# A two-layer MoE trunk: expert weights loaded as 8 KB runs per partition, features folded by four

## The chip, the cores and the metric

The kernel runs on one core of a Trainium2 chip. The metric is the device time of one execution in microseconds (us); the kernel before takes 935.08 us, the median of three runs between 932.46 and 935.89 us.

## The reference, cut to what matters

256 tokens of width 1024 (float32) pass two layers. Each has a token mixer (stick-breaking attention in layer 0, retention in layer 1) and then a mixture of experts (MoE) with 16 experts; every one of the four sublayers is modulated by a conditioning vector and closed by a layer norm:

```python
shift, scale, gate = adaln_params(c, ada_w[i, 1], ada_b[i, 1])      # silu(c) @ w + b, split in 3
h = x * (1.0 + scale) + shift
logits = h @ router_w + router_b                                    # 16 experts in 4 groups of 4
...                                                                 # best group, its top 2, softmax
for e in range(16):
    hidden = silu(h @ w_gate[e]) * (h @ w_up[e])                    # 1024 -> 512
    out = out + combine[:, e:e+1] * (hidden @ w_down[e])            # 512 -> 1024
x = layer_norm(ALPHA * x + (1.0 + gate) * out, ln_g[i, 1], ln_b[i, 1])
```

The weights of all 16 experts are read in each layer: 16 x 3 matrices of 2 MB, 96 MB a layer.

## The kernel before, in words

**Stages.** The program runs stick-breaking attention, MoE of layer 0 (180 to 447 us of the trace), retention and MoE of layer 1 (660 to 918 us). Tokens lie on the 128 partitions in two blocks b. `res` holds the residual.

**An MoE.** Each expert takes up to 64 tokens; the experts are worked in eight pairs p, and both experts of a pair (u = 0, 1) stand in the two column halves of TensorE (`py[64*u:64*u+64]`), so that two matmuls run side by side. For a pair, `gather` picks its tokens out of `xn` with one-hot matmuls (L859), giving their features on the partitions (`xg`, eight tiles of 128 features, modulated by L424 and L425); `up` (matmuls L902) makes the gate and then the up product; L926 and L930 make silu(gate) x up in `mosg`; `turn` (L937) transposes it to `hidT`, four tiles of 128 hidden features; the down product (L957) is made in two halves j of 512 output columns, each in its own `py`; L962 weighs it by the router's weight and the adaLN gate into `moy`, L354 and L355 split that into two float32r parts `moyh` and `moyl`, and `scatter` (L974) puts them back to the token rows by one-hot matmuls, which `accumulate` (L462) adds to `res`. Scatters are held in a list: that of j = 0 is popped at the end of its own pair, that of j = 1 after the next pair's gate product. After pair 1 both are made at once, and `spill` asks with an If (L789, L790) if any expert has more than 64 tokens; only then it loops over the experts.

**Loads.** SyncE's queue (SP) issues nearly all DMAs in the order of the program. `load` (L155 to L161) brings 1 MB into a ring slot as [128 partitions][4][512]: row 128k + p of a 512 x 512 piece goes to partition p, so a partition gets four runs of 2 KB from four places. A pair takes 12 such loads: four each for gate, up and down. The last pair loads its last halves in smaller pieces (`mixed`). A slot is loaded again as soon as its last matmul is done.

**Around it.** `vectors` (L188 to L201) loads the small vectors at the program's start, between the second and the third load of `ada_w`. `ada_part` (L246 to L272) makes the adaLN vectors: L254 multiplies by `ada_w`, L266 turns the row into columns. `logits` transposes `res` (L310) for the router product (L318). `norm` (L486) makes `xn` on ScalarE (ACT), `applied` (L502, L503) scales it into `res`, `gate_row` (L329) and `row_ps` (L212) spread a column vector over all rows.

Of the kernel before, what the change touches and what calls it, by code (L numbers as in the profile page):

```python
# [36 lines left out]
# low part of a phase, tag: (buffers, floats per partition), in the order in which they lie in SBUF  # L37
# [3 lines left out]
# tag: its buffers as (slot of 2048 floats, offset); without an offset the buffer is the whole slot  # L41
# [47 lines left out]
def tile_trunk(ctx, tc, x, c, positions, ada_w, ada_b, ln_g, ln_b, sb_w_in, sb_w_out, ret_w_in, ret_gn_g,  # L89
# [13 lines left out]
    def ps(shape=(P, 512), tag="ps"):  # L103
# [4 lines left out]
            "dy": "t2", "rank": "pc", "ang": "t2", "crow": "sb", "spu": "t2"}  # L108
# [46 lines left out]
    def load(src):  # L155
        tag = state["ring"][state["at"] % len(state["ring"])]
        state["at"] += 1
        t = wp.tile([P, 4, 512], F32, tag="w", name=nm("w")) if tag == "w" else slot(tag, [P, 4, 512])
        if src is not None:
            SY.dma_start(t, src.rearrange("(k p) f -> p k f", p=P))  # L160
        return t  # L161

# [23 lines left out]
    col = keep([P, 176], "col")  # L186

    def vectors():  # L188
# [9 lines left out]
        SY.dma_start(wr, router_w.rearrange("(k p) e -> p k e", p=P))  # L198
# [4 lines left out]
    def gcol(i):  # L203
        return col[:, 96 + 8 * i:104 + 8 * i]

    def bcol(i):
        return col[:, 128 + 8 * i:136 + 8 * i]
# [33 lines left out]
    sums = {}  # L241

    def ada_part(i, j, on_pe):
# [19 lines left out]
        def rest():  # L263
            tp = ps([P, 4, 2], "po" if state["name"] == "RETEN" else "ps")
            for q in range(4):
                T.matmul(tp[:, q, :], e[:, q * P:(q + 1) * P], part if on_pe else ones[:, 0:2], start=(q == 0), stop=(q == 3))  # L266
            V.tensor_tensor(sums[i][:, 4 * j:4 * j + 4], tp[:, :, 0],
                            col[:, 24 * i + 4 * j:24 * i + 4 * j + 4], op=OP.add)
            if j >= 2:
                V.tensor_scalar(sums[i][:, 4 * j:4 * j + 4], sums[i][:, 4 * j:4 * j + 4], 1.0, None, op0=OP.add)  # L270
        return rest

    def ada_mod(i):
# [4 lines left out]
        V.tensor_tensor(mod[:, 8:16], gcol(i - 1), m2[:, 8:16], op=OP.mult)  # L278
        V.tensor_tensor(mod[:, 0:8], bcol(i - 1), m2[:, 8:16], op=OP.mult)
# [17 lines left out]
    def logits(st, ws, side):  # L297
# [5 lines left out]
        with urgent():  # L303
            for b in range(NB):
                for j in range(2):
                    hT = big([P, 4, P], "hT")
                    with tc.issue_after(state["end"]):
                        for q in range(4):
                            k = 4 * j + q
                            T.transpose(zs[b][j][:, q], res[:, b, k * P:(k + 1) * P], ident)  # L310
# [15 lines left out]
    def gate_row(i, tag="ps"):  # L326
        gate = tmp([P, D], "gate", 1)
        for j in range(2):
            A.activation(gate[:, j * 512:(j + 1) * 512], row_ps(sums[i][:, 16 + 4 * j:20 + 4 * j], tag),  # L329
                         AF.Copy)  # L330
# [147 lines left out]
    def norm(i, xn, mom, n=1, ahead=1):  # L478
        parts = [slice(q * D // n, (q + 1) * D // n) for q in range(n)]
        for b, (m, r) in enumerate(mom):  # L480
# [3 lines left out]
            for q in parts:  # L484
                if b < ahead:
                    last = A.activation(xn[b][:, q], res[:, b, q], AF.Identity, scale=r, bias=off)  # L486
                else:
                    last = V.tensor_scalar(xn[b][:, q], res[:, b, q], m, r, op0=OP.subtract, op1=OP.mult)
# [5 lines left out]
    def affine(i, xn, j, g, o):  # L494
        return applied(xn, j, side_row(gcol(i), j, g), side_row(bcol(i), j, o))

    def applied(xn, j, g, o):
        js = slice(j * 512, (j + 1) * 512)

        def apply():  # L500
            for b in range(NB):
                V.scalar_tensor_tensor(res[:, b, js], xn[b][:, js], ALPHA, g, op0=OP.mult, op1=OP.mult)  # L502
# [285 lines left out]
    def spill(l, xn, sc, sh, over, flag, gate):  # L788
        fv = nc.values_load(flag[0:1, 0:1], skip_runtime_bounds_check_because="only compared with zero")  # L789
        with tc.If(fv > 0):  # L790
            hT = big([P, NK, P], "sphT")
            for b in range(NB):
# [6 lines left out]
                with tc.For_i(0, NE, 1) as e:  # L799
                    def dyn(w, r0, c0):  # L800
                        t = big([P, 1, 512], "dy")
                        G.dma_start(t, w[l, bass.ds(e, 1), r0:r0 + P, c0:c0 + 512].rearrange(
                            "e (k p) f -> p (e k) f", p=P))
                        return t

                    def up(w):
                        o = ps()
                        for k in range(NK):
                            t = dyn(w, P * k, 0)
# [27 lines left out]
    def moe(l, i, xn, sc, sh, L, st, after, spare):  # L837
        with tc.issue_after(state["end"]):
            scaled = [affine(i - 1, xn, 1, ps(), ps())]
# [4 lines left out]
        with tc.issue_after(counted):  # L844
            scaled.append(applied(xn, 0, g, side_row(bcol(i - 1), 0, ps(tag="row"))))
# [36 lines left out]
        def both(w, p, rows, js, mixed):  # L882
            w = w[l, 2 * p:2 * p + 2, rows, js]
            if not mixed:
                return [[t[:, f, :] for f in range(4)] for t in (load(w[u]) for u in range(2))]
            ts = [[], []]
            for g in ([[0, 1]], [[2], [3]]):
                t = load(None)
                for n, f in enumerate(g):
                    d = t[:, 2 * n:2 * n + 2 * len(f), :].rearrange("p (u f) c -> p u f c", u=2)  # L890
                    for u in range(2):
                        SY.dma_start(d[:, u], w[u, f[0] * P:f[-1] * P + P, :].rearrange("(f p) c -> p f c", p=P))
                        ts[u].extend(d[:, u, i, :] for i in range(len(f)))
            return ts

        def up(w, p, xg, kt, o=None, mixed=False):
            o = o or ps()
            ts = both(w, p, slice(512 * kt, 512 * kt + 512), slice(0, 512), mixed)
# [19 lines left out]
        for p in range(NE // 2):  # L918
# [7 lines left out]
            A.activation(sgt, pg, AF.Silu)  # L926
# [3 lines left out]
            V.tensor_tensor(sgt, sgt, pu, op=OP.mult)  # L930
# [15 lines left out]
            for j in range(2):  # L946
                js = slice(j * 512, (j + 1) * 512)
                with urgent() if last and j else nullcontext():
                    py = ps()
                    ts = both(moe_w_down, p, slice(0, 512), js, last and j)  # L950
                    for f in range(4):
# [135 lines left out]
```

## Time and profile before

| | us |
|---|---|
| median of three runs | 935.08 (932.46 to 935.89) |
| the profiled execution: span | 928.9 |
| around the span, in the median run | 6.2 |
| TensorE (PE) busy | 884.7 (95% of the span) |
| VectorE (DVE) / ScalarE (ACT) busy | 503.8 / 264.0 |
| DMA | 305.81 MB, mean 329 GB/s |

The span is the time from the first to the last instruction of the profiled execution. The profile gives no device time for that execution itself; the 6.2 us are the difference of the median and the span. A float32 matmul on 512 columns appears as two rows of the trace, a float32r one as one.

### The profile page before, as it was taken

What the parts mean: (1) busy time and instruction counts of PE and PEld (TensorE: products, weight loads), DVE (VectorE), ACT (ScalarE), POOL (GpSimd) and SP (SyncE); (2) the same over time, 40 slices, a digit from 0 to 9 for tenths busy, and PEclk for the clock granted to TensorE, in tenths of its full rate; (3) what the DMA queues carried; (4) which work ended last, traced back from release to release, by engine and by line L of the source; (5) the groups of instructions that cost most, each with busy time, mean ns of one, the idle gap of its engine ahead of it and who ended that gap; (6) DMA issues with size and microseconds to landing.
All of it is one profiled execution on the core that took longest, in us unless ns stands there. A gap on an engine that the chain in (4) does not pass through costs nothing. (4 is left out here: it accounts for less than half of the span.)

```text
span 928.9 us, 11845 instructions
## 1 busy us (share of the span) xinstructions
PE 884.7 (95%) x4687; PEld 552.5 (59%) x4687; DVE 503.8 (54%) x958; ACT 264.0 (28%) x393; POOL 22.1 (2%) x46
## 2 busy tenths in 40 slices
PE   5899999999989999999899999999999899999994
PEld 2598887674434444344778888888944444344431
DVE  1488899635233335333797899748634422343226
ACT  1446646132111111011445434446211111111110
POOL 1000000000000000000000110030000000000000
PEclk9999999999999999999999999999899999999997
DMA  8999998899999999999469878859669999999951
GB/s 305 388 386 386 326 326 305 289 384 378 379 386 386 387 386 387 386 387 386 159 214 346 296 249 309 320 206 350 242 222 373 387 385 386 386 386 386 386 188 46
DMA packets 155378, 305.81 MB, mean 329 GB/s; under 512 B 6521, under 2 KB 6961, under 8 KB 155313
## 3 DMA queue, kind: packets, MB, share of 16 engines
q1 hardware_dynamic: 155312, 304.96, 90.3%
q8 instruction: 39, 0.64, 0.3%
q14 instruction: 27, 0.21, 0.1%
HBM read 303.89 MB, written 1.05 MB: 328 GB/s over the span
## 5 line engine op out<-in xcount | busy, mean ns | idle before, releaser
L902 PE MATMUL ps<-s,xg 128*64 128x512 f32 x544 | 154.4, 603 | 2.5 <-DVEq L790 1.4
L902 PE MATMUL ps<-w,xg 128*64 128x512 f32 x480 | 138.5, 596 | 1.4 <-DVEq L790 1.4
L355 DVE TENSOR_TENSOR wp<-w,wp 128x1024 fp32r<-128x1024 f32 x68 | 82.9, 1221 | 24.1 <-ACT wp L354 24.1
L354 ACT ACTIVATE wp<-w 128x1024 fp32r<-128x1024 f32 x68 | 71.4, 1056 | 81.7 <-PE ps L376 78.2
L902 PEld LDWEIGHTS ps<-s,xg 128*64 128x64 f32 x544 | 45.4, 138 | 73.3 <-issue 68.2
L902 PEld LDWEIGHTS ps<-w,xg 128*64 128x64 f32 x480 | 42.3, 137 | 67.4 <-issue 64.5
L425 ACT ACTIVATE xg<-ps,mod 128x128 f32<-128x128 f32 x64 | 29.3, 457 | 173.7 <-PE ps L859 147.1
L957 PE MATMUL ps<-s,hidT 128*64 128x512 f32 x272 | 75.6, 596 | 2.4 <-ACT xg L425 0.8
L462 DVE TENSOR_TENSOR res<-res,ps 128x512 f32<-128x512 f32 x64 | 41.3, 684 | 67.0 <-PE ps L974 66.7
L259 DVE SCALAR_TENSOR_TENSOR s<-w,cact,s 128x512 f32<-128x512 f32 x104 | 77.1, 747 | 0.8
L930 DVE TENSOR_TENSOR mosg<-mosg,ps 128x512 f32<-128x512 f32 x16 | 11.0, 688 | 114.7 <-PE ps L902 114.7
L859 PEld LDWEIGHTS ps<-oneh,xn 128*128 128x128 f32 x512 | 59.8, 192 | 16.2 <-issue 14.6
L957 PE MATMUL ps<-w,hidT 128*64 128x512 f32 x240 | 67.7, 595 | 1.7 <-DVE hidT L940 1.1
L859 PE MATMUL ps<-oneh,xn 128*128 128x128 f32 x512 | 65.0, 279 | 0.0
L375 PE MATMUL ps<-wp,hh 128*128 128x512 f32 (+1 forms) x144 | 56.6, 394 | 0.0
L376 PE MATMUL ps<-wp,hl 128*128 128x512 f32 x144 | 55.2, 388 | 0.0
L374 PE MATMUL ps<-wp,hh 128*128 128x512 f32 (+1 forms) x144 | 53.4, 397 | 0.7 <-ACT wp L354 0.7
L424 DVE TENSOR_SCALAR xg<-ps,mod 128x128 f32<-128x128 f32 x64 | 26.2, 409 | 50.4 <-ACT xg L425 50.3
L354 ACT ACTIVATE moyh<-moy 128x512 fp32r<-128x512 f32 x32 | 20.1, 630 | 106.8 <-DVE moy L962 106.8
L962 DVE SCALAR_TENSOR_TENSOR moy<-ps,cs,gate 128x512 f32<-128x512 f32 x32 | 24.0, 751 | 48.1 <-PE ps L957 48.1
L957 PEld LDWEIGHTS ps<-s,hidT 128*64 128x64 f32 x272 | 24.0, 137 | 38.3 <-issue 35.6
L926 ACT ACTIVATE mosg<-ps 128x512 f32<-128x512 f32 x16 | 9.6, 597 | 118.3 <-PE ps L902 118.3
(324 smaller groups left out, 1459.6 us busy)
## 6 DMA issues: line engine op xcount, KB each, us to landing
w<-in_ada_w SPq DMA_DIRECT2D x46, 1024.0 KB, 7.4
s<-in_moe_w_gate SPq DMA_DIRECT2D x34, 1024.0 KB, 14.1
s<-in_moe_w_up SPq DMA_DIRECT2D x32, 1024.0 KB, 14.0
w<-in_moe_w_gate SPq DMA_DIRECT2D x30, 1024.0 KB, 14.1
w<-in_moe_w_down SPq DMA_DIRECT2D x30, 1024.0 KB, 13.2
s<-in_moe_w_down SPq DMA_DIRECT2D x30, 1024.0 KB, 13.2
w<-in_moe_w_up SPq DMA_DIRECT2D x28, 1024.0 KB, 13.2
w<-in_ret_w_in SPq DMA_DIRECT2D x24, 1024.0 KB, 7.2
```

Of the source, the lines that this page charges most:

```text
L259: V.scalar_tensor_tensor(e, wt[:, kk, :], cact[:, k:k + 1], e, op0=OP.mult, op1=OP.add)
L354: A.activation(hi, src, AF.Copy)
L355: return V.tensor_tensor(lo, src, hi, op=OP.subtract).ins
L374: T.matmul(dst, lh, rh, start=start, stop=False)
L375: T.matmul(dst, lh, rl, start=False, stop=False)
L376: state["mm"] = T.matmul(dst, ll, rh, start=False, stop=stop).ins
L424: return V.tensor_scalar(dst, src, sc[:, k:k + 1], sh[:, k:k + 1], op0=OP.mult, op1=OP.add).ins
L425: return A.activation(dst, src, AF.Identity, scale=sc[:, k:k + 1], bias=sh[:, k:k + 1]).ins
L462: V.tensor_tensor(res[:, b, js], res[:, b, js], add, op=OP.add)
L859: T.matmul(gp[:, kk, :], xn[b][:, k * P:(k + 1) * P], oneh[:, b].rearrange("p e s -> p (e s)"), start=(kk == 0 and b == 0), stop=(kk == 3 ...
L902: state["mm"] = T.matmul(o[64 * u:64 * u + 64, :], xg[:, k, u * CAP:(u + 1) * CAP], ts[u][kk], start=(k == 0), stop=(k == NK - 1)).ins
L957: state["mm"] = T.matmul(py[64 * u:64 * u + 64, :], hidT[:, f, u * CAP:(u + 1) * CAP], ts[u][f], start=(f == 0), stop=(f == 3)).ins
```

## The change

The gate and up weights of a pair (all but the last pair's up) are loaded with four consecutive matrix rows on one partition: feature 4p + f of a group of 512 lies on partition p, as one run of 8 KB. The contraction of a matmul then runs over every fourth feature, and everything else that meets these features is folded by four in the same way: the columns of scale, shift and norm in the MoE's adaLN vectors (`fcol`, loaded by three more small DMAs and turned by four more transposes), the router's rows, the transposes of `res` (which read every fourth float), `xn`, and the `mosg` that the down product takes. The non-last down products are loaded by whole rows, two rows on a partition as [128][2][1024], and both column halves j are worked in turn from each piece. Both scatters of a pair are held until the whole gate product of the next pair is done. The diff, cut to its core:

```diff
-    def load(src):
+    def load(src, rows="(k p) f -> p k f", shape=(P, 4, 512)):
...
+        if src is not None and rows is None:
+            SY.dma_start(t.rearrange("p f c -> p (f c)"), src)
+        elif src is not None:
+            SY.dma_start(t, src.rearrange(rows, p=P))
...
+    def folded(a, n=4):
+        return a.rearrange("p (f q) -> p q f", q=n)
...
+        wide = big([P, 512], "wide")[0:40, :]
+        for r0, a in ((0, ada_b), (24, ln_g), (32, ln_b)):
+            n = 24 if r0 == 0 else 8
+            SY.dma_start(wide[r0:r0 + n, :], a.rearrange("l s (t f) -> (l s t) f", f=512))
+        cf = ps([P, 4, 40])
+        for q in range(4):
+            T.transpose(cf[:, q, :], folded(wide)[:, q, :], ident[0:40, 0:40])
+        V.tensor_copy(fcol.rearrange("p r q -> p q r"), cf)
...
-                T.matmul(tp[:, q, :], e[:, q * P:(q + 1) * P], part if on_pe else ones[:, 0:2], start=(q == 0), stop=(q == 3))
+                T.matmul(tp[:, q, :], folded(e)[:, q, :] if i % 2 else e[:, q * P:(q + 1) * P],
+                         part if on_pe else ones[:, 0:2], start=(q == 0), stop=(q == 3))
...
-                            T.transpose(zs[b][j][:, q], res[:, b, k * P:(k + 1) * P], ident)
+                            T.transpose(zs[b][j][:, q], folded(res[:, b, 512 * j:512 * j + 512])[:, q, :], ident)
...
+                    last = A.activation(to(xn[b][:, q]), of(res[:, b, q]), AF.Identity, scale=r, bias=off)
...
+                    V.scalar_tensor_tensor(folded(res[:, b, js]), xn[b][:, js].rearrange("p (q f) -> p q f", q=4), ALPHA,
+                                           folded(g), op0=OP.mult, op1=OP.mult)
...
+        def whole(w, p, kt):
+            return [[t[:, f, :] for f in range(4)] for t in
+                    (load(w[l, 2 * p + u, 512 * kt:512 * kt + 512, :].rearrange("(p f) c -> p (f c)", p=P), None)
+                     for u in range(2))]
...
+            sgf = sgt.rearrange("p (q f) -> p f q", q=4)
+            A.activation(sgf, pg.rearrange("p (f q) -> p f q", q=4), AF.Silu)
...
+            if not last:
+                pys = [ps() for _ in cols]
+                for h in range(2):
+                    ts = [load(moe_w_down[l, 2 * p + u].rearrange("(p f) c -> p (f c)", p=P)[:, 2048 * h:2048 * h + 2048],
+                               None, (P, 2, 1024)) for u in range(2)]
+                    for py, js in zip(pys, cols):
+                        for i in range(2):
+                            f = 2 * h + i
+                            for u in range(2):
+                                state["mm"] = T.matmul(py[64 * u:64 * u + 64, :], hidT[:, f, u * CAP:(u + 1) * CAP],
+                                                       ts[u][:, i, js], start=(f == 0), stop=(f == 3)).ins
+                for j in range(2):
+                    weighed(pys[j], cols[j], j)
...
+            for j in range(2 if last else 0):
```

In the changed kernel `load` stands at L155 to L165, the gate and up matmuls at L945, the down matmuls at L1020 and the scatter at L1004. Not in the diff's core: `norm` makes two pieces of 512 for each block instead of one of 1024, the silu and its product are written with a stride of 128 elements, and `spill`'s loop loads folded rows too.

TensorE's order at the change from one pair to the next (pair 2 to pair 3 of the first MoE). L957 is the down product, L902 the next pair's gate, L974 the scatter; `moyh` and `moyl` are the two parts of a half's weighed product. Before:

```order
L957 MATMUL ps_2393<-s_2396,hidT_2338 64x512
L974 MATMUL ps_2412<-moyh_2389,pt_2336 128x512
L974 MATMUL ps_2413<-moyh_2389,pt_2336 128x512
L902 MATMUL ps_2420<-s_2421,xg_2341 64x512
...
L902 MATMUL ps_2420<-s_2423,xg_2341 64x512
L974 MATMUL ps_2412<-moyl_2390,pt_2336 128x512
L974 MATMUL ps_2413<-moyl_2390,pt_2336 128x512
L902 MATMUL ps_2420<-s_2433,xg_2341 64x512
...
L974 MATMUL ps_2445<-moyh_2408,pt_2336 128x512
L974 MATMUL ps_2446<-moyh_2408,pt_2336 128x512
L974 MATMUL ps_2445<-moyl_2409,pt_2336 128x512
L974 MATMUL ps_2446<-moyl_2409,pt_2336 128x512
L902 MATMUL ps_2455<-w_2456,xg_2341 64x512
```

The same place in the changed kernel, where L1020, L945 and L1004 are the down product, the gate and the scatter:

```order
L1020 MATMUL ps_2387<-s_2402,hidT_2350 64x512
L945 MATMUL ps_2424<-s_2425,xg_2353 64x512
...
L945 MATMUL ps_2424<-s_2439,xg_2353 64x512
L1004 MATMUL ps_2449<-moyh_2414,pt_2348 128x512
L1004 MATMUL ps_2450<-moyh_2414,pt_2348 128x512
L1004 MATMUL ps_2449<-moyl_2415,pt_2348 128x512
L1004 MATMUL ps_2450<-moyl_2415,pt_2348 128x512
L1004 MATMUL ps_2457<-moyh_2420,pt_2348 128x512
L1004 MATMUL ps_2458<-moyh_2420,pt_2348 128x512
L1004 MATMUL ps_2457<-moyl_2421,pt_2348 128x512
L1004 MATMUL ps_2458<-moyl_2421,pt_2348 128x512
L945 MATMUL ps_2467<-w_2468,xg_2353 64x512
```

The eight scatter matmuls, which stood in three groups of 2, 2 and 4 around the two halves of the gate product, stand in one group behind it. This holds at the five changes from pair 0 to 1 and 2 to 6; at 6 to 7 the first two groups are joined, and from pair 1 to 2 (the If) nothing moves.

The down product of pair 1, the one before the If, whose two tiles (the first name of a row) are the two column halves. Before:

```order
L957 MATMUL ps_1957<-s_1958,hidT_1921 64x512
...
L957 MATMUL ps_1957<-w_1960,hidT_1921 64x512
L957 MATMUL ps_1976<-s_1977,hidT_1921 64x512
...
L957 MATMUL ps_1976<-s_1979,hidT_1921 64x512
L974 MATMUL ps_1995<-moyh_1972,pt_1919 128x512
```

The same in the changed kernel:

```order
L1020 MATMUL ps_1969<-s_1971,hidT_1933 64x512
...
L1020 MATMUL ps_1970<-w_1973,hidT_1933 64x512
L1020 MATMUL ps_1969<-s_1983,hidT_1933 64x512
...
L1020 MATMUL ps_1969<-s_1985,hidT_1933 64x512
L1020 MATMUL ps_1970<-s_1983,hidT_1933 64x512
...
L1020 MATMUL ps_1970<-s_1985,hidT_1933 64x512
L1004 MATMUL ps_2007<-moyh_1997,pt_1931 128x512
```

The first half was done after 8 of these 16 matmuls and is now done after 12.

The issues on SP's queue at the program's start; before:

```order
L160 DMA w_106<-in_ada_w 128x4x512
L189 DMA s_80<-in_ln_g 32x128
L190 DMA s_80<-in_ln_b 32x128
L191 DMA s_80<-in_ret_gn_g 16x128
L196 DMA con<-in_const 128x436
L197 DMA posi<-in_positions 128x2x1
L198 DMA wr<-in_router_w 128x8x16
L199 DMA rb<-in_router_b 128x16
L160 DMA w_134<-in_ada_w 128x4x512
```

And in the changed kernel:

```order
L162 DMA w_107<-in_ada_w 128x4x512
L197 DMA s_80<-in_ln_g 32x128
L198 DMA s_80<-in_ln_b 32x128
L199 DMA s_80<-in_ret_gn_g 16x128
L207 DMA s_121<-in_ada_b 24x512
L207 DMA s_121<-in_ln_g 8x512
L207 DMA s_121<-in_ln_b 8x512
L212 DMA con<-in_const 128x436
L213 DMA posi<-in_positions 128x2x1
L214 DMA wr<-in_router_w 128x2x64
L215 DMA rb<-in_router_b 128x16
L162 DMA w_145<-in_ada_w 128x4x512
```

Three more DMAs (L207) stand between the second and the third load of `ada_w`. Beyond that SP's order is the same as before.

## Rows read from the trace of the kernel before

**Rows 1.** The page's busy times, and two of the rows of its 40 equal slices (23.2 us each): the DMA engines' share in tenths and the GB/s.

```profile
PE 884.7 (95%) x4687; PEld 552.5 (59%) x4687; DVE 503.8 (54%) x958; ACT 264.0 (28%) x393; POOL 22.1 (2%) x46
...
DMA  8999998899999999999469878859669999999951
GB/s 305 388 386 386 326 326 305 289 384 378 379 386 386 387 386 387 386 387 386 159 214 346 296 249 309 320 206 350 242 222 373 387 385 386 386 386 386 386 188 46
```

**Rows 2.** TensorE's waits over the whole program: what waited for what, us in total, times, longest. The list has 19 rows.

```profile
PE ps L254 <- DMA w<-in_ada_w: 6.4, 5, 4.0
PE ps L266 <- ACT s L261: 5.0, 7, 0.8
PE ps L177 <- DMA s<-in_c: 3.2, 1, 3.2
PE ps L902 <- DVEq L790: 2.8, 2, 1.4
```

**Rows 3.** The page's two groups of gate and up matmuls, and the larger of the two groups of down matmuls: busy us, mean ns of one, and idle time of TensorE just before them with what ended most of it.

```profile
L902 PE MATMUL ps<-s,xg 128*64 128x512 f32 x544 | 154.4, 603 | 2.5 <-DVEq L790 1.4
L902 PE MATMUL ps<-w,xg 128*64 128x512 f32 x480 | 138.5, 596 | 1.4 <-DVEq L790 1.4
...
L957 PE MATMUL ps<-s,hidT 128*64 128x512 f32 x272 | 75.6, 596 | 2.4 <-ACT xg L425 0.8
```

**Rows 4.** The end of the first MoE: the timeline of SP (start, length, how many) with the issue of its last loads; the DMA issues between 396 and 414 us (median us from issue to landing); and the timeline of TensorE with the last eight down matmuls.

```profile
408.92 4.05 SPq L892 DMA_DIRECT2D s<-in_moe_w_down  x5
...
s<-in_moe_w_down SPq DMA_DIRECT2D x4, 256.0 KB, 10.7
...
436.46 1.94 PE L957 MATMUL ps<-s,hidT 128*64 128x512 f32 x8
```

**Rows 5.** The chain of waits through the change from one pair to the next in the second MoE (start us, us, what, how many rows), and from an earlier stretch of the same chain 32 float32 rows in one run.

```profile
778.15 7.02 PE ps L902 x32
...
789.73 7.09 PE ps L957 x32
796.81 0.66 PE ps L974 x2
797.48 3.58 PE ps L902 x16
801.06 0.66 PE ps L974 x2
801.72 3.58 PE ps L902 x16
805.31 1.14 PE ps L974 x4
```

**Rows 6.** The program's start: SP's issues (start, length of the issuing), what SP's queue waited for in the first 13 us, and TensorE's products by the first two loads of `ada_w`, with the idle time before in brackets.

```profile
7.34 0.47 SPq L199 DMA_DIRECT2D rb<-in_router_b  x1
10.18 2.47 SPq L160 DMA_DIRECT2D w<-in_ada_w  x4
...
SPq L160 <- DMA w<-in_ada_w: 2.3, 1, 2.3
SPq L199 <- DMA w<-in_ada_w: 1.3, 1, 1.3
...
7.46 1.94 PE L254 MATMUL ps<-w,cact 128*32 128x512 f32 x8 [4.02 <-DMA w<-in_ada_w]
...
10.20 1.93 PE L254 MATMUL ps<-w,cact 128*32 128x512 f32 x8 [0.45 <-DMA w<-in_ada_w]
```

**Rows 7.** The timelines of VectorE and TensorE before the If of the first MoE.

```profile
260.79 0.69 DVE L355 TENSOR_TENSOR moyl<-moy,moyh 128x512 fp32r<-128x512 f32 x1 [0.70 <-ACT moyh L354]
262.78 0.75 DVE L962 SCALAR_TENSOR_TENSOR moy<-ps,cs,gate 128x512 f32<-128x512 f32 x1 [1.29 <-PE ps L957]
...
264.25 0.73 PE L974 MATMUL ps<-moyh,pt 128*128 128x512 f32 x2 [0.39 <-ACT moyh L354]
265.61 0.74 PE L974 MATMUL ps<-moyl,pt 128*128 128x512 f32 x2 [0.63 <-DVE moyl L355]
267.74 0.65 PE L902 MATMUL ps<-w,xg 128*64 128x512 f32 x2 [1.40 <-DVEq L790]
```

**Rows 8.** Single lines: count, shortest, median and longest ns, first and last start. L289 is a VectorE reduction that reads with a stride of 64 bytes, L876 one that reads 256 consecutive floats. Then two rows of TensorE's timeline with one group each of the transposes of `res` and of the adaLN turning matmuls.

```profile
L289 DVE TENSOR_REDUCE total<-ws x2: 592/597/602, 149.5 to 582.5; 128x32 f32<-128x256 f32 x2
...
L876 DVE TENSOR_REDUCE cs<-row x16: 415/418/425, 223.7 to 902.2; 128x1 f32<-128x256 f32 x16
...
190.87 1.07 PE L310 MATMUL ps<-con,res 128*128 128x128 f32 x8
...
526.88 0.95 PE L266 MATMUL po<-con,s 128*128 128x2 f32 x8
```

**Rows 9.** Busy times by stretch; the last three columns are TensorE's granted clock (a share of full speed), the DMA engines' share and the GB/s. In the first stretch the load of `x` is moved, in runs of 4 KB, in the second expert weights in runs of 2 KB.

```profile
23.50:25.80 2.30, 2.30 (x15) 0.25 (x8) 0.00 (x0) 0.00 (x0) 0.00 (x0) 1.00 1.02 403
...
300.00:302.70 2.70, 2.70 (x13) 1.02 (x10) 0.00 (x0) 0.55 (x1) 0.00 (x0) 1.00 1.05 386
```

**Rows 10.** The stretches behind the If, first of the second MoE, then of the first, in the same columns, and TensorE's timeline with the first eight gate rows behind the If of the second MoE.

```profile
740.60:744.00 3.40, 3.08 (x8) 1.12 (x10) 0.00 (x1) 0.00 (x0) 0.00 (x0) 0.50 1.05 384
...
267.70:276.00 8.30, 8.26 (x40) 3.42 (x42) 0.00 (x0) 0.60 (x1) 0.00 (x0) 1.00 1.05 386
...
740.91 3.46 PE L902 MATMUL ps<-s,xg 128*64 128x512 f32 x8 [1.41 <-DVEq L790]
```

More of the change, by code (lines that the diff above doesn't have):

```diff
@@ L186, in tile_trunk @@
     col = keep([P, 176], "col")
+    fcol = keep([P, 40, 4], "fcol")
     def vectors():
@@ L476, in both_moments, with norm, to, of @@
         return [(mv[:, b, 0:1], r[:, b:b + 1]) for b in range(NB)]
-    def norm(i, xn, mom, n=1, ahead=1):
+    def norm(i, xn, mom, n=1, ahead=1, fold=False):
+        if fold:
+            n = 2
         parts = [slice(q * D // n, (q + 1) * D // n) for q in range(n)]
+        def to(a):
+            return a.rearrange("p (q f) -> p q f", q=4) if fold else a
+        def of(a):
+            return folded(a) if fold else a
         for b, (m, r) in enumerate(mom):
@@ L838, in moe @@
         with tc.issue_after(state["end"]):
[L839 removed]
+            scaled = [affine(i - 1, xn, 1, ps(), ps(), True)]
             gate = gate_row(i)
@@ L844, in moe @@
         with tc.issue_after(counted):
-            scaled.append(applied(xn, 0, g, side_row(bcol(i - 1), 0, ps(tag="row"))))
+            scaled.append(applied(xn, 0, g, side_row(bcol(i - 1), 0, ps(tag="row")), True))
         def gather(p, between):
@@ L884, in both @@
             if not mixed:
-                return [[t[:, f, :] for f in range(4)] for t in (load(w[u]) for u in range(2))]
+                return [[t[:, f, :] for f in range(4)] for t in (load(w[u], "(p f) c -> p f c") for u in range(2))]
             ts = [[], []]
@@ L978, in moe @@
                 held.append(scatter)
-                if j == 1:
-                    with urgent() if last else nullcontext():
+            cols = [slice(0, 512), slice(512, 1024)]
+            if not last:
[12 more added lines that the diff above has]
+            for j in range(2 if last else 0):
+                js = cols[j]
+                with urgent() if j else nullcontext():
+                    py = ps()
+                    ts = both(moe_w_down, p, slice(0, 512), js, j)
+                    for f in range(4):
+                        if j and f == 2:
+                            with tc.issue_after(state["mm"]):
+                                held.pop(0)()
+                        with tc.issue_after(state["mm"]) if j and f == 2 else nullcontext():
+                            for u in range(2):
+                                state["mm"] = T.matmul(py[64 * u:64 * u + 64, :], hidT[:, f, u * CAP:(u + 1) * CAP],
+                                                       ts[u][f], start=(f == 0), stop=(f == 3)).ins
+                    spare[2 + j]()
+                    weighed(py, js, j)
+                if j:
+                    with urgent():
                         held.pop(0)()
@@ L1022, in tile_trunk @@
     with urgent():
-        norm(0, xn, mom, ahead=2)
+        norm(0, xn, mom, ahead=2, fold=True)
     st = stats_tiles(2)
@@ L1042, in tile_trunk @@
     with urgent():
-        norm(2, xn, mom, ahead=2)
+        norm(2, xn, mom, ahead=2, fold=True)
         tc.keep_in_program_order(A.preload_act_table_set("exp_and_others"))
```

99 lines of the change are left out of this document (45 added, 54 removed).

## The prediction, made blind

> **What bounds the kernel now.** I read the page's busy times and slices first. TensorE (PE) is busy for 884.7 of 928.9 us, and through both MoEs (slices 9 to 18 and 31 to 37) the DMA engines are busy too, at 386 GB/s [rows 1]. Two engines look like the bound, so the next view is PE's list of waits: of its 19 rows only two name a DMA, L254 for `ada_w` (5 times, 6.4 us) and L177 (once), and both lines stand in the program's start or the adaLN work [rows 2]. The page's groups agree: the 1024 gate and up rows have 3.9 us of idle time ahead of them, 2.8 of it behind the two Ifs [rows 3]. So PE bounds the MoEs. DMA keeps up by a lead. At the end of the first MoE, five issues end at 412.97 us, the smaller pieces land 10.7 us after their issue, thus at about 423.7, and the last down matmuls that need them start at 436.46: 12.8 us in hand [rows 4]. Only up to about 41 us, before the first attention matmuls, does the program wait for data.
>
> **The loads.** At 386 GB/s 1 MB takes 2.72 us. A run of 4 KB (`x`) showed 403 GB/s, one of 2 KB 386 [rows 9], so 8 KB runs should go at least at 403, 2.60 us. Twelve loads of a pair then take 31.2 us instead of 32.6, and nobody waits for them: value 0. Its bounds: a gain of 21 us if the transfers set the time after all (about 87 loads a MoE back to back, from 186 to 423 us, x 2 x 0.12), and a loss worked out under the rivals.
>
> **The scatter's place.** The change from pair to pair takes 7.09 + 0.66 + 3.58 + 0.66 + 3.58 + 1.14 = 16.71 us in the chain [rows 5]. In the changed order the 32 down rows and the 32 gate rows stand in runs of 32, and each such run takes 7.02 [rows 5]; here it is followed by eight scatter rows. Four rows take 1.14 and two 0.66, so a further row is 0.24 and eight are 2.10. Together 7.02 + 7.02 + 2.10 = 16.14: 0.57 less. This is the cost of passing four times more often between float32 and float32r work. Ten changes (0 to 1 and 2 to 6, twice) give -5.7; where 6 to 7 joins two groups of two, 0.66 + 0.66 - 1.14 = 0.18 twice: -0.4. Nothing is late behind it: both `moy` halves have the 7 us of gate work to be weighed and split in. What VectorE then has to add, four additions in a row instead of two and two, meets an engine busy for 54% of the span. Term: -6.1; bounds -6.1 and 0 if the switch is not what costs.
>
> **The If.** After pair 1 the scatters follow at once. PE waits 0.39 and 0.63 us there for the split of the second half and 1.40 for the If's answer [rows 7]. The first half is now ready after 12 of 16 down matmuls instead of 8, so its product on VectorE starts with the fourth quarter of the 7.02 us, at about 255.6 + 5.3 = 260.9. It takes 0.75, ScalarE's rounding about 0.7 (the bracket of the 260.79 row), VectorE's rest 0.69, until 263.1. The second half's product, which started at 262.78, waits behind it on VectorE: +0.37. Twice: +0.7 (bounds 0 and 1.0).
>
> **The start.** SP's queue issues its 12th DMA (L199) at 7.34, when the first load of `ada_w` has landed (L254 starts at 7.46), and the 13th, the third load of `ada_w`, at 10.18 (L254 starts at 10.20) [rows 6]. So a DMA waited for the one eight places ahead, and three more in between change who waits: the 12th is now the constants, the 13th the positions, and behind it stand the router's weights, the router's bias and only then `ada_w`. Each issue takes 0.47 [rows 6], so it comes at 10.18 + 3 x 0.47 = 11.6, and the data that PE waits for are 1.4 us later: +1.4. Bounds: 0, if later loads make it up, and +2.0. The four transposes and the copy on VectorE lie in idle time: PE sat 4.02 us before its first product [rows 6].
>
> **Reads by every fourth float.** The transposes (four groups of eight, 1.07 us each) and the odd adaLN turning matmuls (twelve groups of eight, 0.95 each) [rows 8] read PE's operands with a stride of 16 bytes: 15.7 us in all. No such read of PE is in the trace. The nearest row is VectorE's reduction with a stride of 64 bytes, 597 ns against 418 for as many consecutive floats [rows 8], 1.43 times, which would be +6.7. It writes 32 results instead of one and its stride is four times as long, and part of the adaLN groups stand in front of waits for ScalarE [rows 2]. I take a third, +2.2; bounds 0 and, at twice the time, +15.7. [...]
>
> The strided writes and reads of ScalarE and VectorE (norm, silu, its product, `applied`) are off PE's path: both engines are busy for less than 55% [rows 1]. Without that cover, `mosg`'s product in front of `turn` would cost 0.3 us a pair (0.69 x 0.43), some 5 us in all; it has about 2 us to spare in all but the last pair, so I put nothing there.
>
> **Sum.** -6.1 + 0.7 + 1.4 + 2.2 + 0 = -1.8 us. Against the profiled span of 928.9 this is 927.1; with the 6.2 us that lie between span and median, 933.3 us.
>
> **The rivals.**
>
> *The fold is free and the start catches up:* -6.1 + 0.7 = -5.4, 929.7 us. [...] Against it: the VectorE row.
>
> *The strided reads decide (slower):* PE's reads by every fourth float, in the transposes ahead of the router and the turning matmuls inside attention and retention. Without them the sum is -4.0; from a factor of 1.25 on the change loses, at a factor of 2 it is -4.0 + 15.7 = +11.7, 946.8 us. For it: PE is busy at 95%, so little hides there. [...]
>
> *Long runs move slower, and the transfers become the bound:* the lead of 12.8 us shrinks by 5 x 0.57 with the shorter pairs; spread over 87 loads that leaves 0.11 us a load. Below 371 GB/s (2.83 us) the DMA is late; at 3.0 us it would cost 87 x 0.28 - 10 = 14 us a MoE, +28 - 1.8, about 961 us. Against it: the 4 KB row went faster, not slower.
>
> *The transfers set the time already:* 87 x 2 x 0.12 = 21 us less, 912 us, more if 8 KB go beyond 403 GB/s. For it: a DMA share above 1.0. Against it: rows 2 to 4 show no wait.
>
> One more uncertainty is the granted clock. [...]
>
> **How the numbers follow.** About 0.5%, 4.7 us, is what a measurement of this kernel can tell from no change. The forecast has a chance of 0.49; its own terms and the clock spread it from 929 to 939, which gives 0.08 faster, 0.37 within, 0.04 slower. The free fold has 0.25, as it ends near the bound half of it counted faster and half within. The strided reads have 0.13: 0.09 slower, 0.04 within. Slow transfers 0.05, slower. Transfers that set the time 0.08, faster. Sums: faster 0.08 + 0.13 + 0.08 = 0.29, within 0.37 + 0.12 + 0.04 = 0.53, slower 0.04 + 0.09 + 0.05 = 0.18. The range from 926.5 to 941 holds the forecast, the free fold and the strided reads up to a factor of about 1.6; outside are the fast transfers and half of the two slow cases.
>
> **What would show it.** Right: loads of the experts at 400 GB/s or more in the MoEs with no DMA in PE's waits; one run of 64 float32 rows and one group of eight scatter rows of about 2.1 us at a change of pairs; the third load of `ada_w` issued at about 11.6 us and attention starting about 1.4 us later; gaps at the If of 1.40 us and a scatter that starts 0.37 us later; the L310 and L266 groups at 1.1 to 1.3 us. Wrong: a group of eight at 1.6 us or more, PE waiting for `moe_w` loads, MoEs that are shorter by more than 3 us each, or a scatter group that takes over 2.6 us.

## The result and the profile after

The changed kernel takes 942.59 us (median of 4 runs, 941.71 to 943.82) against 933.77 us of the kernel before in the same comparison: 1.0103 times as long by the record's estimate, 95% interval 1.0079 to 1.0126 (the medians alone give 1.0094). The forecast was 933.3 us, with a range of 926.5 to 941.0. The profiled execution spans 941.7 us, 12.8 more than that of before. Each run's own span shows that a device time is the span plus 1.6 to 2.0 us, so the execution profiled before was one of about 930.9 us, a quick one; of the 12.8 us, 8.8 stand in the medians. The diff has one more edit, which the description of the change leaves out: `dynamic_dma_scratch_size=8192` where the program is built. No run tries it alone; turn_pad72 below has it too and is faster than the kernel before.

The page of the changed kernel: busy times, two rows of slices as in [rows 1], the gate and up matmuls as in [rows 3], and the two groups that make `mosg`.

```profile
PE 890.5 (95%) x4691; PEld 561.3 (60%) x4691; DVE 510.9 (54%) x959; ACT 277.9 (30%) x397; POOL 23.1 (2%) x46
...
DMA  8999788797999999999259968949759979999911
GB/s 278 390 386 378 279 299 306 274 414 280 381 421 408 421 421 419 421 394 345 70 193 355 314 205 291 344 148 358 290 210 384 422 321 421 421 420 420 402 41 45
...
L945 PE MATMUL ps<-s,xg 128*64 128x512 f32 x544 | 153.3, 603 | 6.3 <-issue 3.8
L945 PE MATMUL ps<-w,xg 128*64 128x512 f32 x480 | 139.0, 602 | 1.4 <-DVEq L823 1.4
...
L974 DVE TENSOR_TENSOR mosg<-mosg,ps 128x512 f32<-128x512 f32 x16 | 16.9, 1053 | 114.6 <-PE ps L945 114.6
...
L970 ACT ACTIVATE mosg<-ps 128x512 f32<-128x512 f32 x16 | 17.4, 1090 | 110.5 <-PE ps L945 104.2
```

The 8 KB runs move at 421 GB/s where 2 KB runs moved at 386, and that buys nothing: the matmuls of the MoEs still wait for no load. What is new in these rows is 3.8 us of idle time ahead of L945 put down to "issue", which is nothing that the profile shows. TensorE's list of waits says the same:

```profile
PE ps L272 <- DMA w<-in_ada_w: 8.2, 5, 3.9
...
PE ps L945 <- issue: 3.8, 1, 3.8
...
PE ps L945 <- DVEq L823: 2.8, 2, 1.4
```

The start, to be read against [rows 6]: SP's issues, then TensorE's third product by `ada_w`, here and in the kernel before.

```profile
5.58 0.29 SPq L207 DMA_DIRECT2D s<-in_ln_b  x1
7.25 0.36 SPq L212 DMA_DIRECT2D con<-in_const  x1
10.19 0.39 SPq L213 DMA_DIRECT2D posi<-in_positions  x1
...
11.64 2.56 SPq L162 DMA_DIRECT2D w<-in_ada_w  x4
...
17.18 1.93 PE L272 MATMUL ps<-w,cact 128*32 128x512 f32 x8 [2.28 <-DMA w<-in_ada_w]
```

```profile
15.37 1.94 PE L254 MATMUL ps<-w,cact 128*32 128x512 f32 x8 [0.59 <-DMA w<-in_ada_w]
```

The third load of `ada_w` is issued at 11.64 instead of 10.18, behind the 13th DMA and two more, as worked out. That third product starts 1.81 us later than in the trace of before.

The chain through a change of pairs in the second MoE, against [rows 5]:

```profile
804.77 7.09 PE ps L1020 x32
811.86 6.87 PE ps L945 x32
818.73 2.04 PE ps L1004 x8
820.77 7.02 PE ps L945 x32
```

Down, gate and scatter take 7.09 + 6.87 + 2.04 = 16.00 us instead of 16.71, and the next down product starts 27.52 us after this one, against 28.30 in the chain of before: 0.78 less for each of ten changes. From pair 6 to 7 it is 27.54 us for 27.87, 0.33 less in each MoE.

The loss is elsewhere. Single lines of the changed kernel, against [rows 8]: the weight loads of the adaLN turning matmuls, one group of them and one of the transposes of `res` in TensorE's timeline, and ScalarE's norm.

```profile
L284 PEld LDWEIGHTS ps<-con,s x72: 188/329/332, 59.9 to 181.1; 128*128 128x128 f32 x72
...
535.97 1.80 PE L284 MATMUL po<-con,s 128*128 128x2 f32 x8
...
200.03 1.18 PE L328 MATMUL ps<-con,res 128*128 128x128 f32 x8
...
L515 ACT ACTIVATE xn<-res,off,rs x8: 1282/1293/1322, 204.0 to 681.5; 128x512 f32<-128x512 f32 x8
```

A group of eight turning matmuls takes 1.80 us, not 0.95. With TensorE's rows of the two traces matched in order, the lag of the changed kernel grows by 0.72 to 0.96 us at eleven of the twelve groups (at the first by more, as the clock falls behind it), and by 5.0 us over the six groups of the retention: 0.83 on average. The transposes only go from 1.07 to 1.18.

The slower norm shows once. In front of the second MoE VectorE waits for ScalarE, whose four norm pieces come first there, and TensorE then waits for VectorE:

```profile
684.41 0.19 DVE L781 TENSOR_TENSOR ex<-ex,top 128x32 f32<-128x32 f32 x1 [1.22 <-ACT ex L770]
...
686.08 0.18 PE L797 MATMUL ps<-sel,counts 128*128 128x32 bf16 x1 [0.84 <-DVE sel L793]
```

The kernel before has no idle time at this place, and neither has turn_strided below, at full clock.

### The profile page after: what moved, and what is told of

Read it like the earlier page. It is cut to its first block, busy times and chain, and to the rows that moved or that the text cites. A ratio compares the mean times of both kernels' runs of the same rounds, so it can differ in the third digit from the quotient of the medians.

```text
span 941.7 us, 11891 instructions
## 1 busy us (share of the span) xinstructions
PE 890.5 (95%) x4691; PEld 561.3 (60%) x4691; DVE 510.9 (54%) x959; ACT 277.9 (30%) x397; POOL 23.1 (2%) x46
## 5 line engine op out<-in xcount | busy, mean ns | idle before, releaser
L945 PE MATMUL ps<-s,xg 128*64 128x512 f32 x544 | 153.3, 603 | 6.3 <-issue 3.8
L945 PE MATMUL ps<-w,xg 128*64 128x512 f32 x480 | 139.0, 602 | 1.4 <-DVEq L823 1.4
L945 PEld LDWEIGHTS ps<-s,xg 128*64 128x64 f32 x544 | 46.7, 139 | 80.4 <-issue 75.5
L945 PEld LDWEIGHTS ps<-w,xg 128*64 128x64 f32 x480 | 42.8, 139 | 72.2 <-issue 69.8
L974 DVE TENSOR_TENSOR mosg<-mosg,ps 128x512 f32<-128x512 f32 x16 | 16.9, 1053 | 114.6 <-PE ps L945 114.6
L1020 PE MATMUL ps<-w,hidT 128*64 128x512 f32 x240 | 67.7, 595 | 1.7 <-DVE hidT L984 1.3
L1020 PE MATMUL ps<-s,hidT 128*64 128x512 f32 x208 | 60.6, 595 | 1.7 <-DVE hidT L984 1.1
L970 ACT ACTIVATE mosg<-ps 128x512 f32<-128x512 f32 x16 | 17.4, 1090 | 110.5 <-PE ps L945 104.2
L1020 PEld LDWEIGHTS ps<-s,hidT 128*64 128x64 f32 x208 | 18.4, 137 | 33.2 <-issue 29.7
## 6 DMA issues: line engine op xcount, KB each, us to landing
w<-in_moe_w_gate SPq DMA_DIRECT2D x30, 1024.0 KB, 14.1
s<-in_moe_w_down SPq DMA_DIRECT2D x30, 1024.0 KB, 10.4
```

The costliest lines, as they stand in the source:

```text
L945: state["mm"] = T.matmul(o[64 * u:64 * u + 64, :], xg[:, k, u * CAP:(u + 1) * CAP], ts[u][kk], start=(k == 0), stop=(k == NK - 1)).ins
L1020: state["mm"] = T.matmul(py[64 * u:64 * u + 64, :], hidT[:, f, u * CAP:(u + 1) * CAP], ts[u][:, i, js], start=(f == 0), stop=(f == 3)).ins
```

## The experiments

The theory after the comparison had two parts: TensorE's loads of weights by every fourth float cost 12 x 0.73 = 8.8 us, and the late start about 2. (The 0.73 us a group were read somewhat low; the rows give 0.83.) Rivals were the long runs themselves, the slower ScalarE and VectorE, and, for the gain, that it was not the scatter's place. All times below are medians; a ratio is to the kernel before, run on the same chip beside it. The median of the kernel before differs from set to set (932.55 to 933.77 us), so where two sets are compared, the difference of each to its own kernel before counts.

**turn_strided**, the kernel before with six groups strided:

```diff
+                T.matmul(tp[:, q, :], e.rearrange("p (f q) -> p q f", q=4)[:, q, :] if (i, j) in strided else e[:, q * P:(q + 1) * P], part ...
```

> The kernel before, in which only six of the twelve groups of adaLN turning matmuls that belong to the MoEs (columns 2 to 5 of layer 0's, 4 and 5 of layer 1's) read their 128x128 operand by every fourth float; the columns come out in another order, so that scale and gate are permuted. Theory (TensorE's weight loads with a stride of 16 bytes are the loss): each group goes from 0.95 to about 1.7 us, +0.73 us each, +4.4 us in all, 936 to 940 us against 933.8. Rival (the loss is in the start, the long runs or VectorE and ScalarE): within 1 us of the kernel before.

Measured: 936.81 us, 1.0038 (1.0011 to 1.0065), 4.3 us over 932.55: the theory's number, though the interval, 1.0 to 6.1 us, ends near the rival's 1 us. In the trace the lag grows by 4.7 us over the six groups.

**turn_plain**, the changed kernel with VectorE folding the row, so that TensorE reads consecutive floats:

```diff
+                elif k == 7 and i % 2:
+                    e, s = big([P, 512], "E"), e
+                    V.scalar_tensor_tensor(e.rearrange("p (q f) -> p q f", q=4), folded(wt[:, kk, :]), cact[:, k:k + 1], folded(s), ...)
...
-                T.matmul(tp[:, q, :], folded(e)[:, q, :] if i % 2 else e[:, q * P:(q + 1) * P], ...
+                T.matmul(tp[:, q, :], e[:, q * P:(q + 1) * P], ...
```

> The changed kernel, in which VectorE's last product of each of the twelve groups writes its row already folded into a second buffer, so that the turning matmuls read consecutive floats again. Theory (strided weight loads of TensorE): 12 x 0.73 = 8.8 us less than the changed kernel, about 934 us; VectorE's product is some 0.4 us longer. Rival (the loss is elsewhere): within 1 us of 942.6.

Measured: 928.53 us, 0.9967 (0.9946 to 0.9988), faster than both kernels: 14.1 us less than the changed kernel, 12.8 by the differences to their own kernels before. That is more than the theory's 8.8 and than the 10 us of twelve groups at 0.83. Part of the rest is the clock. In the changed kernel it averaged 0.57 of full speed in two stretches ahead of the first MoE (0.50 from 102.1 to 105.4 us and from 204.5 to 211.2), the first right behind a strided group; in turn_plain it stayed at 1.00 up to 735 us. Changed kernel first, turn_plain second (the third number from the end is the clock):

```profile
101.90:105.90 4.00, 4.00 (x21) 3.99 (x21) 3.84 (x6) 1.59 (x3) 0.00 (x0) 0.57 0.78 277
...
204.00:212.00 8.00, 8.00 (x44) 8.00 (x44) 4.19 (x21) 5.06 (x7) 0.00 (x0) 0.57 1.01 420
```

```profile
17.00:200.00 183.00, 172.24 (x1098) 139.46 (x1099) 135.32 (x230) 86.03 (x115) 1.11 (x2) 1.00 0.96 354
200.00:735.00 535.00, 522.05 (x2715) 328.30 (x2713) 312.22 (x608) 163.33 (x238) 20.50 (x35) 1.00 0.86 333
```

From the first transpose of `res` to the first `gather` of the first MoE, where the clock fell for 6.8 us, the changed kernel takes 14.48 us and turn_plain 11.68. From pair 5 to 6 of that MoE it takes 28.75 us and turn_plain 27.53, as the matmuls there stand in another order. How much of the clock's fall follows from the strided loads was not separated.

**turn_every2** reads every second float instead.

> As turn_strided, the same six groups, but TensorE reads every second float (8 bytes apart) instead of every fourth; the columns of scale and gate are permuted in another way. [...] Rival (any stride costs): about 330 ns as with every fourth float. [...]

The one execution took 934.83 us, too few for a verdict on the time; the loads are what it was made for. The weight loads of turn_strided, then of turn_every2, each with one strided group (only some of the 72 loads are strided):

```profile
L267 PEld LDWEIGHTS ps<-con,s x72: 188/192/332, 57.2 to 175.0; 128*128 128x128 f32 x72
...
126.47 1.80 PE L267 MATMUL ps<-con,s 128*128 128x2 f32 x8
```

```profile
L267 PEld LDWEIGHTS ps<-con,s x72: 187/192/197, 57.7 to 172.7; 128*128 128x128 f32 x72
...
126.97 0.99 PE L267 MATMUL ps<-con,s 128*128 128x2 f32 x8
```

At most 332 ns with a stride of 16 bytes and at most 197 with 8, where consecutive floats took 192: the rival's 330 ns for any stride is out, and so is a cost that grows evenly with the stride. Reading every fourth float, a load takes 1.7 times as long (329 ns) and a group 1.9 times (1.80 us for 0.95). Why this stride costs and 8 bytes do not, no run shows.

**wide_late** moves the three small DMAs behind the attention's constants and their transposes behind the first adaLN vectors.

> The changed kernel with the three extra small DMAs issued behind the load of the attention's constants and turned after the first adaLN vectors, instead of ahead of the third load of ada_w. Theory of the start (three issues in a queue that waits for the load eight places ahead): the third load is issued at 10.2 us again and the whole program ends 1.8 to 2.5 us earlier, about 940.5 us. Rival (the delay is made up later, or comes from the wider router load): within 0.7 us of 942.6.

Measured: 939.57 us, 1.0089 (1.0067 to 1.0111). That is 3.0 us less than the changed kernel's median, but 7.0 us over its own kernel before where the changed kernel is 8.8 over its own: 1.8 us less, a difference that the two intervals do not separate. The trace shows the cause: the third load of `ada_w` is issued at 10.10 again, and the third product starts at 15.35 instead of 17.18.

**scatter_held**, the kernel before with the scatter alone moved:

```diff
-                if j == 1:
-                    with urgent() if last else nullcontext():
+                if j == 1 and last:
+                    with urgent():
                         held.pop(0)()
```

> The kernel before with only the scatter moved: both scatters of a pair are held until the next pair's gate product is done; loads and features as before. Theory (passing between float32 and float32r matmuls costs TensorE time): 6 to 8 us less than the kernel before, 926 to 928 us. Rival (the MoEs gained by the longer runs, not by the scatter's place): within 1.5 us of 933.8.

Measured: 930.99 us, 0.9980 (0.9958 to 1.0002): inconclusive. The trace shows the gain, 27.52 us from one down product to the next with the kernel before's loads, and things that ate a part of it: a lower clock ahead of the first MoE (the stretch is shown for this kernel, then for the kernel before) and an idle time behind the second If. Besides, the gate product from pair 6 to 7 is cut after one matmul in both MoEs here, a kind of cut that pad72_split prices below.

```profile
192.00:203.00 11.00, 11.00 (x71) 11.00 (x72) 4.95 (x26) 4.63 (x8) 0.00 (x0) 0.69 1.05 386
...
743.19 3.22 PE L902 MATMUL ps<-s,xg 128*64 128x512 f32 x13 [1.64 <-issue]
```

```profile
192.00:203.00 11.00, 11.00 (x100) 10.88 (x100) 5.89 (x29) 5.28 (x9) 0.00 (x0) 1.00 1.05 386
```

**short_runs** brings the same floats to the same places with four DMAs of 2 KB runs in place of each 8 KB one.

> The changed kernel with every 8 KB load issued as four DMAs of 2 KB runs that put the same floats in the same places. Theory (the transfers are hidden, the length of a run is worth nothing): the loads fall back from 421 to about 386 GB/s and the time stays within 1.5 us of 942.6; the idle time behind the second If stays, as it comes from the code. Rival 1 (8 KB packets delay the code): that idle time falls below 1.5 us, some 3 us faster. Rival 2 (the long runs paid in the MoEs): 3 us slower or more.

Measured: 942.78 us, 1.0104 (1.0066 to 1.0143), the time of the changed kernel. Sixty microseconds of the first MoE, changed kernel first and short_runs second (TensorE's busy time is the second number):

```profile
320.00:380.00 60.00, 59.82 (x317) 27.77 (x314) 26.44 (x71) 9.54 (x19) 0.00 (x0) 1.00 1.01 420
```

```profile
320.00:380.00 60.00, 59.82 (x314) 27.18 (x311) 26.45 (x71) 9.40 (x18) 0.00 (x0) 1.00 1.04 384
```

420 or 384 GB/s, TensorE is equally busy, and where the matmuls stand in the same order a pair takes 27.52 to 27.53 us in both, from one down product to the next. The equal totals alone would not show it: the idle time at the second If is longer here, 6.2 us for 3.8, and the two changes from pair 5 to 6 are 2.9 us shorter, as their order differs. That the idle time stays shows that it does not come from the long packets either.

**plain_late** and **plain_pad.** The idle time at the second If had appeared in every kernel with new matmuls on TensorE ahead of it. One queue of instruction transfers keeps step with TensorE: 39 transfers of 16 KB each, one for every 238 instructions that TensorE executed in the kernel before, on average. They are taken for its code; the page's row on their queue (packets, MB, share):

```profile
q8 instruction: 39, 0.64, 0.3%
```

Behind the second If the next one began 3.5 to 3.9 us after the branch in every trace, and took 1.1 us. The new theory: the branch lands where little loaded code is left.

> The changed kernel with both edits at once: turning matmuls that read consecutive floats, and the three small DMAs issued later. If the two losses are separate, their gains add: 928.5 - 3.0 = 925.5 us, and the attention starts within 0.7 us of where it starts in the kernel before. If the earlier start is eaten by another wait, it stays at 928 to 929 us.

> The kernel of plain_late with 24 more instructions on TensorE, twelve repeats of the very first small transpose, which write the same values in idle time. Theory (behind the If of the second MoE TensorE runs dry because the branch lands a few instructions before the end of the code that is loaded, and waits for the next 16 KB): with the code moved by 24 instructions the idle time of 4 to 6 us there is gone or under 2 us, and the kernel is 3 to 5 us faster than plain_late. Rival (the code's transfer stands behind the 8 KB packets of the weights, wherever the branch lands): the idle time stays above 3.5 us and the time within 1 us of plain_late.

Measured: plain_late 931.52 us (0.9983, 0.9960 to 1.0007), plain_pad 932.73 us (0.9995, 0.9971 to 1.0020). Both misses. plain_late starts its third product 1.96 us earlier than turn_plain, but ends later: the order of its matmuls between pairs 5 and 6 of the first MoE came out differently (an up product cut after one matmul; 30.76 us from one down product to the next for 27.53), and the clock fell ahead of the first MoE (14.48 us there for 11.68). It separates nothing. In plain_pad the idle time stayed at 6.1 us, though now ahead of the end of the branch instead of behind it. Counting TensorE's executed instructions up to the branch gave the reason: 24 more was too few.

**before_pad, plain_pad72, turn_pad72**:

```diff
-    T.transpose(colp[:, 0:8], crow, ident[0:8, 0:8])
+    for _ in range(14):
+        T.transpose(colp[:, 0:8], crow, ident[0:8, 0:8])
```

with 37 in place of 14 in the other two.

> The kernel before with only 26 more instructions on TensorE, thirteen repeats of the first small transpose, which write the same values while TensorE has nothing to do. Theory (the branch of the second If lands so near the end of the loaded code that TensorE waits for the next 16 KB; TensorE's 7752nd instruction is the branch in the kernel before, its 7777th to 7805th where it stalls): idle time of 4 to 5 us more at the second If and a kernel 4 to 5 us slower, 937 to 938 us. Rival (the stall belongs to the long runs or to the changed MoE): no idle time beyond 1.8 us there and within 1 us of the kernel before.

> The kernel of plain_late with 72 more such instructions in place of 24. [...] Rival: the idle time of 6 us stays.

> The kernel of turn_plain (turning matmuls that read consecutive floats) with the same 72 instructions. Theory: 4 us faster than turn_plain, about 924.5 us, faster than both kernels of this study; rival: 928.5 us as before.

Measured: before_pad 937.63 us, 1.0057 (1.0036 to 1.0078), 4.5 us over the kernel before; plain_pad72 925.23 us, 0.9909 (0.9878 to 0.9940); turn_pad72 925.26 us, 0.9914 (0.9888 to 0.9941). TensorE's first matmuls behind the second If in before_pad, then in plain_pad72:

```profile
746.99 3.68 PE L903 MATMUL ps<-s,xg 128*64 128x512 f32 x8 [6.09 <-issue]
```

```profile
739.65 4.05 PE L955 MATMUL ps<-s,xg 128*64 128x512 f32 x17 [1.45 <-DVEq L833]
```

6.09 us against 1.45, the If's own wait. By the differences to their own kernels before, plain_pad72 gains 6.0 us on plain_late, more than the 4.3 to 4.7 us by which the gap in the table below is shorter, as no stretch of low clock follows its If, where in plain_late one of 6.8 us did (the mean granted clock of the profiled execution is 0.991 for 0.983). All kernels, by the number of TensorE's executed instructions ahead of that branch, counted in the traces:

| number | kernel | longest gap between starts of matmuls there, us |
|---|---|---|
| 7752 | before, turn_every2 | 1.8 |
| 7752 | turn_strided | 1.9, idle for 1.36 after 13 rows |
| 7769 | scatter_held | 2.7, idle for 1.64 after five rows |
| 7777 | changed | 4.4, after one row |
| 7778 to 7781 | before_pad, wide_late, turn_plain, plain_late | 6.1 to 6.5 |
| 7799, 7805 | short_runs, plain_pad | 6.6, 6.5 |
| 7836 to 7853 | pad72_split, turn_pad72, plain_pad72 | 1.8 |

The later the branch, the fewer rows run before the stall (13, five, one, none), until the branch itself stalls; from 7836 on the stall is gone, and there a transfer of code had come 5 to 7 us ahead of the branch. before_pad shows the stall with nothing else changed. That the end of the loaded code is what TensorE waits for is inferred from these places and from the transfers' times.

**pad72_split** cuts the scatter into groups again (`held.pop(0)()` behind both `weighed`).

> The kernel of plain_pad72 with the scatter split again: the first of a pair's two scatters is popped at the end of its own pair, so that the eight matmuls stand in groups of 2, 2 and 4 around the next gate product, as in the kernel before. Theory (passing between float32 and float32r matmuls costs TensorE 0.78 us a change of pairs, as the chains of the kernel before and the changed one show): 16.7 us instead of 15.9 at a change of pairs and 7 to 8 us slower than plain_pad72, about 932.5 us. Rival (a shorter change of pairs is given back elsewhere, as scatter_held alone won only 1.6 us): less than 3 us slower than plain_pad72.

Measured: 942.78 us, 1.0106 (1.0069 to 1.0143), 17.5 us over plain_pad72, over twice the theory. The chain at its change of pairs:

```profile
799.14 7.09 PE ps L1030 x32
806.23 0.66 PE ps L1014 x2
806.89 6.15 PE ps L955 x26
813.04 0.66 PE ps L1014 x2
813.70 1.86 PE ps L955 x6
815.56 1.12 PE ps L1014 x4
```

Here the gate's 16 matmuls are cut after 13. The matmuls of the two column halves start in twos (their rows 0.00 to 0.01 us apart in the kernel before's timeline from 797.4 us), and an odd cut leaves one alone on each side of it: 6.15 + 1.86 = 8.01 us for the gate, where the even cut of the kernel before took 3.58 + 3.58 = 7.16. So a change of pairs takes 17.54 us against 16.00, ten of them 15.4, and the end moved by all of that and a little more. The rival, that a shorter change is given back, is out. What going between float32 and float32r costs by itself does not come out of this run, since the uneven halves add to it; scatter_held's trace shows it.

## Why the prediction was wrong

| term | forecast, us | shown, us | from |
|---|---|---|---|
| scatter's place | -6.1 | -8.5 | 10 x 0.78 + 2 x 0.33, chain of waits |
| the If | +0.7 | +0.3 | below |
| start | +1.4 | +1.8 | third product; wide_late |
| reads by every fourth float | +2.2 | +10.4 | 12 x 0.83 + 4 x 0.11; turn_strided |
| norm, silu and products, strided | 0 | +0.8 | wait ahead of the second MoE |
| loads | 0 | 0 | short_runs |
| code behind the second If | not seen | +4.5 | before_pad |
| sum | -1.8 | +9.3 | measured +8.8 |

**The step that failed is the size of the strided reads.** The prediction put them at +2.2 us and they cost about +10.4. The row that it went by, VectorE's 1.43 times, was itself too low (a turning group takes 1.9 times), and taking a third of it was argued from the shape of that row, not from a row of TensorE. The term's own bounds, 0 and +15.7, do hold what came. The rival "the strided reads decide" had the place and the mechanism, and its chance of 0.13 was too small; that its 946.8 us at a factor of 2 lie near the measured 942.6 is partly luck, as it has the transposes at double time too and nothing of the code. Nearly all the loss is in the turning matmuls, where a load of 128 columns serves a matmul on 2 (loads of 192 ns went to 329). In the transposes the loads went from 140 ns to 209 and the matmuls, on 128, only from 272 to 283: they probably cover the loads.

**A term was missing.** The prediction read from the order that only four transposes were added to TensorE and put them at nothing, since TensorE was idle. It did not ask what more instructions do to the place of the code. Without these 4.5 us the measured time would be about 938 (an estimate), inside the range that ends at 941.0: it took both errors to leave it. A row of the page of the kernel before could have raised the question: 39 instruction transfers on q8, 0.64 MB.

**Right:** what bounds the kernel (TensorE, by the three views) and so the worth of the loads; their speed, 421 GB/s for at least 403; the start, where the waits for the DMA eight places ahead, as [rows 6] show them, gave the issue at 11.6, and it came at 11.64; the scatter, which is worth somewhat more since the gate run ahead of it is also shorter (6.87 for 7.02). At the If the first half does come later, but from the first scatter row to the gate's first row it is 5.20 us for 5.07 at the second If (747.08 to 752.28 us in TensorE's timeline, 735.84 to 740.91 before): waits of 0.59 + 0.43 replace 0.39 + 0.63. (The prediction's own figures there add up to 263.04, which is 0.26 us late and not 0.37.)

**Put at nothing.** ScalarE and VectorE were slower than supposed (`mosg` 1090 and 1053 ns for 597 and 688; the norm 8 x 1.29 us for 4 x 1.23; the one size forecast was 0.43 more for `mosg`'s product). The prediction put nothing there because both engines are busy for less than 55%, an average. It held inside the MoEs, where a pair takes 27.52 us with the slower `mosg`, and failed ahead of the second MoE, where the norm's 0.84 us reach TensorE. This was not tried alone. Nor was the granted clock, which the forecast's spread of 929 to 939 us counts in: no run shows its share of the time. What the traces show in its place are single stretches: eight gate rows in 3.46 us behind the second If of the kernel before, at a clock of 0.50 [rows 10], where eight down rows took 1.94 at 1.00 [rows 4], and 14.48 us for 11.68 ahead of the first MoE.

plain_pad72 and turn_pad72 end at the same time although the first starts its third product 1.5 us earlier: from pair 5 to 6 of the first MoE it takes 30.74 us, turn_pad72 27.52. What stays open is why the order of the matmuls comes out differently there, and how much of the clock's fall in the changed kernel follows from the strided loads.

## What to carry to other kernels

Before folding a layout, look for every weight load of TensorE that will then read every fourth float: it cost most here where a wide load serves a narrow matmul (0.83 us for a group of eight, 0.11 for eight transposes), and another engine with time to spare can write the folded row instead (turn_plain, 12.8 us less than the changed kernel). Here faster transfers, 421 GB/s for 386, were worth nothing, as no matmul of the changed kernel's MoEs waited for a load, and the layout that they need cost about 10.4 us on the engine that bounds the kernel. After any edit that adds instructions ahead of a branch, look at the first idle time behind it: a few microseconds there may come from the place of the code (4.5 in before_pad), and a number of harmless instructions more can remove them (72 in turn_pad72, 925.26 us for turn_plain's 928.53).

## What the runs showed of the hardware

- In the adaLN turning matmuls TensorE's load of 128 x 128 floats took 192 ns from consecutive floats (before, L266) or every second one (turn_every2, L267, at most 198), and 329 from every fourth (changed, L284). In the transposes of `res` it took 140 ns from consecutive floats (before, L310) and 209 from every fourth (changed, L328).
- ScalarE on 512 floats took 1293 ns reading every fourth float (changed, the norm, L515), 1090 writing `mosg` with a stride of 512 bytes (changed, L970) and 597 writing it without a stride (before, L926).
- With 26 instructions more on TensorE ahead of the branch of the second If, the kernel before took 4.5 us more (before_pad). The stall has a window of 29 to 83 instructions (branches at numbers 7777 to 7805 stalled for 3.8 us or more; 7752 for 1.4 at most, 7836 not at all); one transfer of 16 KB came on q8 for every 238 instructions that TensorE executed (before). That the branch stalls at the end of the loaded code is inferred.
- A gate product of 16 matmuls in column halves, cut after 13, took 8.01 us (pad72_split), where the even cut took 7.16 (before): 0.85 us more.
- Going between float32 and float32r matmuls four times less at a change of pairs saved 0.78 us: 27.52 us from one down product to the next (scatter_held) for 28.30 (before).
